# RWKV units in pairs, with one substitution in blocks of 16 for the two of a pair

## The chip, the cores and the metric

The program runs on one core of one Trainium2 chip. The metric is device time in microseconds (us) of one execution. A core has five engines with an instruction queue each, which they work through in order: TensorE (PE, matrix products), VectorE (DVE), ScalarE (ACT), GpSimd (POOL) and SyncE (SP), from which most DMAs are issued. Engines wait for each other by semaphores.

## What is computed

One inference step of a trunk of two layers on 1088 columns: 1024 of a prompt and 8 sequences of 8 samples. Layer 0 mixes by an S5 and a gated DeltaNet, layer 1 by RWKV-7; after each stands a SwiGLU feed-forward part. What matters here is layer 1, cut to this:

```python
def rwkv7_scan(r, decay, k, v, a, b, s0):
    def step(state, inp):
        r_t, w_t, k_t, v_t, a_t, b_t = inp
        sa = jnp.einsum("bhvk,bhk->bhv", state, a_t)
        state = (state * w_t[:, :, None, :] + sa[..., None] * b_t[:, :, None, :]
                 + v_t[..., None] * k_t[:, :, None, :])
        return state, jnp.einsum("bhvk,bhk->bhv", state, r_t)
...
for layer in range(DEPTH):
    ...                       # mixer, then
    x = x + mix.astype(x.dtype)
    h = rmsnorm(x, prm["norm_ffn"][layer])
    x = x + swiglu(h, prm["ffn_w_gate"][layer], prm["ffn_w_up"][layer], prm["ffn_w_down"][layer]).astype(x.dtype)
```

The kernel computes the recurrence in chunks of 64 columns. Within a chunk it needs the inverse of a unit lower triangular 64x64 matrix for each head.

## The kernel before

Every large product goes through `mm` (L322), which splits both factors into a high and a low part and adds three products. The work goes over two halves of the columns. In order of the code: layer 0's first parts, then for each half its tail (output projection `po`, feed-forward products `pg` and `pd`) and layer 1's projections (`pj`); then, for each half, layer 1's output projection and feed-forward tail.

The recurrence of layer 1 is cut into 32 **units** of two heads each: eight head pairs `ft` in four segments `si` of the columns (the last of 320 columns with the samples, the others of 256). I count them in the order of the code, 0 to 31: units 0 to 7 (`si` 0) are called between the projections of the first half, 8 to 15 (`si` 1) behind them, 16 to 23 between those of the second half and 24 to 31 behind. A unit has three parts:

- the **front** (L1550 to L1660): it loads its rows, computes decays, writes `AR`, `BK`, `XV`, `BG` and the chunk matrices `MB`;
- the **inverse** (L155 to L261): the diagonal blocks of 16 are cut out (`D`, L174), go through DRAM (`dA`) into a layout with one block per partition (`L`), are inverted there by a **substitution** of 15 steps with two DVE instructions each (L186, L188), go back through DRAM (`dT`, `Tc`), and from `tt` (L203) on are put together to the inverses `TT` of 64 (last write L259);
- the **back** (L1662 to L1733): for each of four chunks in turn PE, DVE and ACT hand `pa`, `X` (L1685), `pu` and `pb` to each other; then the output `py` is normed to `yo` (L1730) and stored, and read again by the next tail.

Tiles come from pools with a fixed number of buffers. `AR`, `XV`, `BG` and `MB` have two each, so two units can be under way; `TT` has two; the banks `qi` (inverse), `qc` (the back's chunk steps) and `qy` one each. The projections of a half take `qi` and `qc` too (`banks`, L1396).

The order on each engine is set by a scheduler when the kernel is built: it goes by the order of the code and by its own estimate of when inputs are ready. So the units of `si` 1 lie among the tail of the second half of layer 0 (1400 to 2100 us of the profile), and those of `si` 2 and 3 among projections and the tail of layer 1's first half (2330 to 3175 us). On the chip each engine keeps to the order it was given.

Of the kernel before, what the change touches and what calls it, by code (L numbers as in the profile page):

```python
# [8 lines left out]
F32 = mybir.dt.float32  # L9
# [3 lines left out]
OP = mybir.AluOpType  # L13
# [3 lines left out]

T = 1088
NP = 1024
CW = 272  # L20
NCH = [(c, CW) for c in range(0, T, CW)]

# [82 lines left out]
class Kern:  # L105
# [49 lines left out]
    def inverse(self, gp, ps, dr, A, wd, nu, ns, sgn, tag, pb=2, own=False, TT=None):  # L155
# [1 line left out]

        nc, v = self.nc, self.nc.vector  # L160
        nl = 8 * nu + ns
        op = OP.subtract if sgn > 0 else OP.add
        dA = dr.tile([nu + 1, 8, 256], F32, name="dA", tag="dA%d" % wd)
        size = {"mk": 320, "L": 256, "T": 256, "tt32": 160, "Y32": 160}
        kin = {"Y32": "L", "tt32": "T"}
        two = [lambda n, i=i: gp.tile([128, size[kin.get(n, n)] if own else 320], F32, name=n,
                                      tag="i" + kin.get(n, n) if own else "inv%d" % i, bufs=1) for i in range(2)]
        D = gp.tile([128, nu + 1, 16], F32, name="D", tag="invTc", bufs=1 + own)
        for R, n in ((slice(0, 64), nu + 1 if ns else nu), (slice(64, 128), nu)) if wd == 128 else ((slice(0, 128), nu),):
            mk = two[1]("mk").rearrange("p (u b i) -> p u b i", b=4, i=16)[R, 0:n]  # L170
# [4 lines left out]
        nc.sync.dma_start(dA[0:nu].rearrange("u b (j i) -> (b j) u i", i=16), D[:, 0:nu])  # L175
        if ns:
            nc.sync.dma_start(dA[nu, 0:ns].rearrange("b (j i) -> (b j) i", i=16), D[0:16 * ns, nu])
        L = two[0]("L")[:8 * nu + 8, :256].rearrange("p (a b) -> p a b", b=16)
        nc.sync.dma_start(L[:nl], dA.rearrange("u b (j i) -> (u b) j i", i=16)[:nl])
        T = two[1]("T")[:8 * nu + 8, :256].rearrange("p (a b) -> p a b", b=16)  # L180
        v.tensor_copy(T[:nl], self.i16[:nl])
        m = gp.tile([8 * nu + 8, 64], F32, name="Tm", tag="invm", bufs=1)
        for j in range(15):
            n = 15 - j
            mm = m[:nl, :(j + 1) * n].rearrange("p (c i) -> p c i", i=n)
            v.tensor_mul(mm, L[:nl, j:j + 1, j + 1:16].to_broadcast([nl, j + 1, n]),  # L186
                         T[:nl, 0:j + 1, j:j + 1].to_broadcast([nl, j + 1, n]))
            v.tensor_tensor(T[:nl, 0:j + 1, j + 1:16], T[:nl, 0:j + 1, j + 1:16], mm, op=op)  # L188
        dT = dr.tile([nu + 1, 8, 256], F32, name="dT", tag="dT%d" % wd)
        nc.sync.dma_start(dT.rearrange("u b x -> (u b) x")[:nl], T[:nl].rearrange("p c i -> p (c i)"))  # L190
        Tc = gp.tile([128, nu + 1, 16], F32, name="Tc", tag="invTc", bufs=1 + own)
        nc.sync.dma_start(Tc[:, 0:nu], dT[0:nu].rearrange("u b (c i) -> (b c) u i", i=16))
        TS = None
# [16 lines left out]
        C = [slice(32 * b % wd, 32 * b % wd + 32) for b in range(4)]  # L210
# [17 lines left out]
        if TT is None:  # L228
            TT = gp.tile([128, nu, 128], F32, name="TT", tag="invTT", bufs=1)
            nc.gpsimd.memset(TT, 0.0)  # L230
        TT = TT[:, 0:nu]
# [47 lines left out]
    def open(self, ctx, width, tmps, **kw):  # L279

        self.dp = self.dx = ctx.enter_context(self.tc.tile_pool(name="dense", bufs=1, **kw))
        self.width, self.tmps = width, tmps
# [286 lines left out]
class S5:  # L569


    L = 8
    NK = 136
# [632 lines left out]
class RWKV:  # L1206
# [53 lines left out]
    def open(self, ctx):  # L1260

        K, nc, tc = self.K, self.K.nc, self.K.tc
        self.dl = self.dr.tile([288, T], F32, name="dl", bufs=1)
        self.dk, self.drr, self.dv, self.dth, self.dta, self.dg = (
            self.dr.tile([8, 128, T], F32, name=n, bufs=1) for n in ("dk", "drr", "dv", "dth", "dta", "dg"))
        self.dks = {}
        self.ps = ctx.enter_context(tc.tile_pool(name="rps", bufs=2, space=PSUM, side="right"))
        self.gp = ctx.enter_context(tc.tile_pool(name="rww", bufs=2, side="right"))
        self.consts(self.cp)
        self.H = self.cp.tile([128, 8, 64], F32, name="Hs")  # L1270
        nc.gpsimd.memset(self.H, 0.0)

        self.Q = self.cp.tile([128, 4, 2, 64], F32, name="Q")
        nc.gpsimd.memset(self.Q, 0.0)

        self.TT = [self.gp.tile([128, 5, 128], F32, name="TT%d" % i, bufs=1) for i in range(2)]
        self.turn = False
        for t in self.TT:
            nc.gpsimd.memset(t, 0.0)
        self.halo = self.cp.tile([128, 2, 8], F32, name="halo")  # L1280
        nc.vector.memset(self.halo[:, 0], 0.0)

    def projections(self, s, x, shift0, w1, a1, g1, lw2, wk, wr, wv, unit,
                    norms, wk0):

# [152 lines left out]
        for j, wt, dst, more in ((0, wr, self.drr, {1: (0,), 2: (1,), 3: (2, 3), 4: (4, 5), 5: (6, 7)}), (3, wv, self.dv, {})):  # L1438
            hs = [mix(j, i) for i in range(2)]
            if j == 3:  # L1440
                banks = banks[:2]
            for m in range(6):
                w = K.weight(wt[m])
                for i in range(2):
                    one(dst, m, w, hs[i], i)
                for ft in more.get(m, ()):
                    second(ft)
                if j == 3:
                    unit(m)
                if j == 0 and m == 0:  # L1450
                    lora(*loras[5])
                    second = self.second(s, lw2)
                if j == 0 and m == 0:
                    for i, (c, cn) in enumerate(chunks):
                        pt = self.bank("qp")[:16, :cn]
                        for y, (b, n) in enumerate(blocks[i]):
                            nc.tensor.transpose(pt[:, b:b + n], ko[:n, 3 * i + y], K.ident[:n, :n])
                        t = K.tmp("kt")[:16, :cn]
                        nc.scalar.copy(t, pt)
                        nc.sync.dma_start(dks[:, c:c + cn], t)  # L1460
            ws = [K.weight(wt[m]) for m in (6, 7)]
            for i in range(2):
                for m in (6, 7):
                    one(dst, m, ws[m - 6], hs[i], i)
        for m in (6, 7):
            unit(m)
# [68 lines left out]

    def start(self, ft, si, s0, sfin, dy):

        nc, gp = self.K.nc, self.gp
        self.sfin, self.dy = sfin, dy
        S0 = None  # L1540
        if self.SEG[si][2]:
            S0 = gp.tile([128, 8, 64], F32, tag="S0", name="S0", bufs=1)
            nc.sync.dma_start(S0, s0[ft])
        return self.unit(ft, si, si // 2, S0)

    def unit(self, ft, si, s, S0):
        K, nc, gp, HR = self.K, self.K.nc, self.gp, self.HR
        v = nc.vector
        t0, W, smp = self.SEG[si]
        NU, C = 4, 5 if smp else 4  # L1550
        ts = slice(t0, t0 + W)
# [5 lines left out]
        def new(name, tag="up"):  # L1557
            return gp.tile([128, 320], F32, tag=tag, name=name, bufs=RING[tag])[:, :W]
# [64 lines left out]
        pb = ptile("pb")[:, :W]  # L1623
# [7 lines left out]
        MB = gp.tile([128, 5, 64], F32, tag="u_MB", name="MB", bufs=2)  # L1631
        groups = [(0, 4, self.mk)] + ([(4, 1, self.mks)] if smp else [])

        def turned(src, dst):
            for c0, n, mk in groups:
                pt = self.ps.tile([128, 4, 2, 64], F32, tag="q0", name="pt", bufs=2)
                for c in range(n):
                    nc.tensor.transpose(pt[:, c].rearrange("p a t -> p (a t)"),
                                        src[:, c0 + c, 0:2].rearrange("p a t -> p (a t)"), ident)
                nc.scalar.copy(dst[:, c0:c0 + n], pt[:, :n])  # L1640
# [17 lines left out]
                v.tensor_mul(AR[KR, g, hl], pg[KR, :n, 0], mb(KR, 0))  # L1658
                v.tensor_mul(BG[:, g, 1, hl], pg[:, :n, 1], mb(slice(0, 128), 1))
        turned(BK, BG[:, :, 0])  # L1660
        self.turn = not self.turn
        TT, _ = K.inverse(gp, self.ps, self.dr, MB, 64, C, 0, -1.0, "qi", 1, True, self.TT[self.turn])  # L1662

# [4 lines left out]
        pa, pu, pb = pc[:, 0:2], pc[:, 2], pc[:, 3:5]  # L1670
# [7 lines left out]
        two = lambda t: t.rearrange("p a t -> p (a t)")  # L1678
        for u in range(NU):
# [10 lines left out]
            for hl, R in enumerate(HR):  # L1690
                n = XV[R, u + 1, hl] if u + 1 < NU else H[R, NU]
# [29 lines left out]
        for p in parts:  # L1721
            nc.gpsimd.tensor_mul(yc[p], yc[p], wide(rs, p))
            for j in range(p[1].start, p[1].stop):
                n = p[0].stop
# [3 lines left out]
        yo = new("yo", "ul")  # L1728
        v.scalar_tensor_tensor(yo, pT, col(self.lnw), bv, op0=OP.mult, op1=OP.add)
        v.scalar_tensor_tensor(yo, yo, col(self.lnb), g, op0=OP.add, op1=OP.mult)  # L1730
        if si == 3 and ft == 7:
            return yo
        nc.sync.dma_start(self.dy[ft][:, ts], yo)  # L1733

    def sample(self, ft, c, AR, BG, XV, TT, Pe, S0, py):

# [380 lines left out]
```

## Time and profile before

| what | value |
|---|---|
| three runs, median (lowest to highest) | 3689.62 us (3682.62 to 3697.84) |
| the profiled execution, time and span | 3691.23 us, 3689.5 us |
| busy in the span: PE, DVE, ACT, POOL | 92%, 65%, 38%, 28% |
| chain that ended last, by engine | PE 54%, DVE 26%, DMA 12% |

The span is from the first to the last instruction of the profile. A busy PE is not PE at its peak: the records of matmuls that follow each other overlap. An idle engine costs nothing unless the end hangs on it, so the stretches are looked at one by one.

### The profile page before, as it was taken

How to read it: one execution, taken by the hardware profiler on the slowest of the kernel's cores; microseconds unless marked ns; L12 is line 12 of the kernel's file. 1: busy time of each engine (PE TensorE's matmuls, PEld its weight loads, DVE VectorE, ACT ScalarE, POOL GpSimd, SP SyncE). 2: the span in 40 equal slices, each digit the busy share in tenths (PEclk: the TensorE clock that was granted, in tenths of full speed). 3: DMA queues.
4: the chain of work that ended last, by engine and by line, in shares of the span. 5: the costliest groups of instructions: out<-in, count | busy, mean ns of one | idle time of the engine just before them, and what ended most of it. 6: DMA issues, size and time to landing. Idle time of an engine off the chain costs nothing.

```text
span 3689.5 us, 77380 instructions
## 1 busy us (share of the span) xinstructions
PE 3379.0 (92%) x29894; PEld 3171.2 (86%) x29894; DVE 2394.0 (65%) x6834; ACT 1390.8 (38%) x3264; POOL 1041.0 (28%) x1037
## 2 busy tenths in 40 slices
PE   7889999999997889999999898898988989899998
PEld 6879888989997888899889888888887877799997
DVE  7886888754448556776666673577778888344344
ACT  3333333323224454444443454443443444222222
POOL 3222133223216450111010142334333332122221
PEclk8989987999998899999999999989999999899998
DMA  3434453445554585344443456722322324322322
GB/s 102 95 87 120 96 177 104 130 132 188 186 174 132 176 292 161 111 143 150 153 130 114 135 167 221 238 86 87 87 82 84 102 79 135 105 69 75 92 81 66
DMA packets 387552, 474.36 MB, mean 129 GB/s; under 512 B 142312, under 2 KB 305896, under 8 KB 387184
## 3 DMA queue, kind: packets, MB, share of 16 engines
q1 hardware_dynamic: 364144, 447.13, 39.8%
q10 hardware_dynamic: 23040, 22.29, 1.8%
q8 instruction: 235, 3.85, 0.4%
q14 instruction: 133, 1.09, 0.1%
HBM read 344.32 MB, written 123.79 MB: 127 GB/s over the span
## 4 chain that ended last, share of the span: by engine, by line
PE 54%; DVE 26%; DMA 12%; issue 3%; ACT 3%; SPq 1%; POOL 1%; DVEq 0%; ACTq 0%; POOLq 0%
PE pg L322 20%; PE pd L322 10%; PE pj L322 5%; PE po L322 4%; PE pi L322 3%; DVE T L188 3%; DVE Tm L186 3%; DVE mx L1350 1%; DMA raw<-in_wd 1%; DMA dT<-T 1%; DMA L<-dA 1%; DMA rkb<-dks 1%; DMA Tc<-dT 1%; DVE x L534 1%; DVE Z L800 1%
## 5 line engine op out<-in xcount | busy, mean ns | idle before, releaser
L322 PE MATMUL pg<-hi,wh 128*128 128x288 f32 (+1 forms) x2816 | 833.8, 296 | 23.8 <-DVE s L511 15.5
L322 PE MATMUL pg<-lo,wh 128*128 128x288 f32 (+1 forms) x2816 | 830.9, 295 | 4.4 <-DVE lo L409 3.5
L322 PE MATMUL pg<-hi,wl 128*128 128x288 f32 (+1 forms) x2816 | 827.8, 294 | 1.2 <-POOL wl L309 1.2
L309 POOL TENSOR_TENSOR wl<-raw,wh 128x1024 fp32r<-128x1024 f32 (+3 forms) x205 | 483.1, 2358 | 903.5 <-ACT wh L305 791.5
L322 PEld LDWEIGHTS pg<-hi,wh 128*128 128x128 f32 x2816 | 540.7, 192 | 32.9 <-DVE s L511 19.1
L322 PEld LDWEIGHTS pg<-lo,wh 128*128 128x128 f32 x2816 | 540.8, 192 | 12.4 <-DVE lo L409 5.2
L322 PEld LDWEIGHTS pg<-hi,wl 128*128 128x128 f32 x2816 | 540.2, 192 | 3.3 <-POOL wl L309 1.4
L305 ACT CAST wh<-raw 128x1024 fp32r<-128x1024 f32 (+3 forms) x309 | 313.2, 1014 | 362.7 <-PE pg L322 99.6
L322 PE MATMUL pd<-ah,wdh 128*128 128x256 f32 (+1 forms) x1280 | 387.2, 303 | 20.3 <-DVE x L534 16.5
L322 PE MATMUL pd<-ah,wdl 128*128 128x256 f32 (+1 forms) x1280 | 373.5, 292 | 5.9 <-DMA wdl<-low_wd 5.9
L322 PE MATMUL pd<-al,wdh 128*128 128x256 f32 (+1 forms) x1280 | 371.9, 291 | 0.0
L322 PEld LDWEIGHTS pd<-ah,wdh 128*128 128x128 f32 x1280 | 243.8, 190 | 32.0 <-DVE x L534 18.2
L322 PE MATMUL pj<-hi,wh 128*128 128x256 f32 (+1 forms) x768 | 235.5, 310 | 18.1 <-ACT hi L408 7.7
L322 PEld LDWEIGHTS pd<-ah,wdl 128*128 128x128 f32 x1280 | 243.8, 190 | 9.1 <-DMA wdl<-low_wd 7.6
L322 PEld LDWEIGHTS pd<-al,wdh 128*128 128x128 f32 x1280 | 244.2, 191 | 0.4
L322 PE MATMUL pj<-hi,wl 128*128 128x256 f32 (+1 forms) x768 | 232.2, 307 | 12.7 <-DMA wl<-low_wr 7.5
L322 PE MATMUL pj<-lo,wh 128*128 128x256 f32 (+1 forms) x768 | 235.2, 308 | 8.7 <-DVE lo L409 6.8
L534 DVE TENSOR_TENSOR x<-x,pd 128x256 f32<-128x256 f32 (+1 forms) x384 | 162.4, 426 | 92.0 <-PE pd L322 88.5
L305 ACT CAST wdh<-raw 128x384 fp32r<-128x384 f32 (+1 forms) x224 | 111.2, 497 | 258.6 <-PE pd L322 161.2
L322 PE MATMUL pi<-hi,wh 128*128 128x272 f32 x640 | 191.5, 299 | 5.0 <-ACT us L1818 3.5
L186 DVE TENSOR_TENSOR Tm<-L,T 32x15 f32<-32x15 f32 (+8 forms) x600 | 161.1, 268 | 47.6 <-DMA L<-dA 34.6
L322 PE MATMUL pi<-lo,wh 128*128 128x272 f32 x640 | 190.2, 297 | 0.0
(643 smaller groups left out, 8008.2 us busy)
## 6 DMA issues: line engine op xcount, KB each, us to landing
raw<-in_wg SPq DMA_DIRECT2D x88, 512.0 KB
raw<-in_wup SPq DMA_DIRECT2D x88, 512.0 KB
raw<-in_wd SPq DMA_DIRECT2D x192, 192.0 KB
low_wg<-wl SPq DMA_DIRECT2D x22, 512.0 KB
low_wup<-wl SPq DMA_DIRECT2D x22, 512.0 KB
wl<-low_wg SPq DMA_DIRECT2D x22, 512.0 KB
wl<-low_wup SPq DMA_DIRECT2D x22, 512.0 KB
raw<-in_win SPq DMA_DIRECT2D x20, 512.0 KB
```

The costliest lines, as they stand in the source:

```text
L186: v.tensor_mul(mm, L[:nl, j:j + 1, j + 1:16].to_broadcast([nl, j + 1, n]), T[:nl, 0:j + 1, j:j + 1].to_broadcast([nl, j + 1, n]))
L188: v.tensor_tensor(T[:nl, 0:j + 1, j + 1:16], T[:nl, 0:j + 1, j + 1:16], mm, op=op)
L305: nc.scalar.copy(wh, raw)
L309: (lo or nc.gpsimd).tensor_sub(wl, raw, wh)
L322: self.nc.tensor.matmul(ps, a[k], b[:, c:c + cn], start=i == 0, stop=i == last)
L534: v.tensor_add(x[m][:, c:c + cn], x[m][:, c:c + cn], ps)
L800: v.tensor_add(o, o, m1)
L1350: v.scalar_tensor_tensor(t, xx[k][:, c:c + cn], self.vec[:, j, k:k + 1], x[k][:, c:c + cn], op0=OP.mult, op1=OP.add)
```

## The change

`inverse` is cut into `diagonals`, `substitute` and `inverted`; for the DeltaNet the three are called in a row as before. A unit becomes a generator that stops behind `diagonals`. `start` runs the front of an even unit up to there and keeps it; at the odd one it runs that front too, then the rest of the even unit (which does the substitution for both: 64 or 80 partitions in place of 32 or 40) and the rest of the odd one. The pairs are (0, 1), (2, 3) and so on. The numbers of buffers stay as they are.

```diff
         dA = dr.tile([nu + 1, 8, 256], F32, name="dA", tag="dA%d" % wd)
+        self.diagonals(gp, dA, A, wd, nu, ns, own)
+        dT = dr.tile([nu + 1, 8, 256], F32, name="dT", tag="dT%d" % wd)
+        self.substitute(gp, dA, dT, 8 * nu + ns, sgn, own)
+        return self.inverted(gp, ps, dT, A, wd, nu, ns, sgn, tag, pb, own, TT)
...
+    def substitute(self, gp, dA, dT, nl, sgn, own):
...
-        T = two[1]("T")[:8 * nu + 8, :256].rearrange("p (a b) -> p a b", b=16)
+        T = two[1]("T")[:, :256].rearrange("p (a b) -> p a b", b=16)
         v.tensor_copy(T[:nl], self.i16[:nl])
-        m = gp.tile([8 * nu + 8, 64], F32, name="Tm", tag="invm", bufs=1)
+        m = gp.tile([128, 64], F32, name="Tm", tag="invm", bufs=1)
...
     def start(self, ft, si, s0, sfin, dy):
...
-        return self.unit(ft, si, si // 2, S0)
+        unit = self.unit(ft, si, si // 2, S0)
+        next(unit)
+        if ft % 2 == 0:
+            self.other = unit
+            return
+        list(self.other)
+        return next(unit, None)
...
         turned(BK, BG[:, :, 0])
-        self.turn = not self.turn
-        TT, _ = K.inverse(gp, self.ps, self.dr, MB, 64, C, 0, -1.0, "qi", 1, True, self.TT[self.turn])
+
+        if ft % 2 == 0:
+            self.dA, self.dT = (self.dr.tile([2 * C, 8, 256], F32, name=n, bufs=2) for n in ("dA", "dT"))
+        pair, dT = slice(C * (ft % 2), C * (ft % 2) + C), self.dT
+        K.diagonals(gp, self.dA[pair], MB, 64, C, 0, True)
+        yield
+        if ft % 2 == 0:
+            K.substitute(gp, self.dA, dT, 16 * C, -1.0, True)
+        TT, _ = K.inverted(gp, self.ps, dT[pair], MB, 64, C, 0, -1.0, "qi", 1, True, self.TT[ft % 2])
```

In the changed kernel's order lines are numbered anew: L341 is `mm`; L235 to L271 are the inverse's products; L1663 and L1674 are products of the front; L1713, L1718 and L1721 are the back's chunk steps, L1757 its last transposes; L379 and L395 belong to the norm.

PE, end of layer 0's second tail, before. `pd` is the last feed-forward product, `ss` and `bc` are sums for the norm, and `pj` is the first projection of layer 1's second half:

```order
L322 MATMUL pd<-ah,wh 128x288
L322 MATMUL pd<-al,wh 128x288
L322 MATMUL pd<-ah,wl 128x288
L360 MATMUL ss<-sq,one_65 32x72 x32
L376 MATMUL bc<-rst,selq 128x72 x4
L322 MATMUL pj<-hi,wh 128x288 x2
L322 MATMUL pj<-lo,wh 128x288
L322 MATMUL pj<-hi,wl 128x288
```

All units up to 15 stand ahead of these rows. In the changed kernel 48 `pj` stand within 90 rows of the last `pd`, and then come 123 rows without one, of which these are the last, with the 49th `pj` behind them (`py`, `pc` with 128x64 and so on are unit 14's back and, in `py` from 20702 to 20758, unit 15's inverse):

```order
L263 MATMUL py_20564<-t_20519,MB 32x32 x8
L271 MATMUL py_20575<-tt_20557,Y_20563 32x32 x8
L1718 MATMUL pc<-X,TT_13426 128x64
L235 MATMUL py<-t_20702,MB 32x16 x16
L1721 MATMUL pc<-XV,BG 128x128
L239 MATMUL py<-Y_20704,tt 32x16 x16
L1713 MATMUL pc<-XV,AR 128x128
L263 MATMUL py_20747<-t_20702,MB 32x32 x8
L1718 MATMUL pc<-X,TT_13426 128x64
L271 MATMUL py_20758<-tt_20740,Y_20746 32x32 x8
L1721 MATMUL pc<-XV,BG 128x128
L341 MATMUL pj<-hi,wh 128x288
```

What moved: most of the backs of units 10 to 13, and the fronts and inverses of units 12 to 15, stand behind the last `pd`; the 49th `pj` stands behind unit 15's inverse, whose bank `qi` it takes.

PE, end of the tail of layer 1's first half, before. `po` is the output projection of the second half; `pT`, `pk`, `pcr` and `py` are the end of unit 30 and the sample part of unit 31:

```order
L322 MATMUL pd<-ah,wh 128x256
L322 MATMUL pd<-al,wh 128x256
L322 MATMUL pd<-ah,wl 128x256
L360 MATMUL ss<-sq,one_65 32x64 x32
L376 MATMUL bc<-rst,selq 128x64 x4
L1725 MATMUL pT<-ident,yc 128x128 x2
L1725 MATMUL pT<-ident,yc 128x64
L1744 MATMUL pk<-AR,S_34889 64x16 x16
L1750 MATMUL pcr<-ident,rT 64x64 x2
L1761 MATMUL py<-ident,rT 64x128
L376 MATMUL bc<-rst,selq 128x64 x4
L322 MATMUL po<-hi,wh 128x288
```

And now, some 120 rows behind the last `pd` (`pk`, `pcr`, `pcs` are sample parts of unit 29, `py` with x20 are unit 30's inverse):

```order
L1777 MATMUL pk<-AR,S_33190 64x16 x16
L1783 MATMUL pcr<-ident,rT 64x64 x2
L1794 MATMUL py<-ident,rT 64x128
L1789 MATMUL pcs<-XV,AR 64x64 x2
L341 MATMUL po<-hi,wh 128x288 x2
L341 MATMUL po<-lo,wh 128x288
L341 MATMUL po<-hi,wl 128x288
L341 MATMUL po<-lo,wh 128x288
L341 MATMUL po<-hi,wl 128x288
L235 MATMUL py<-t_33440,MB 32x16 x20
L239 MATMUL py<-Y_33442,tt 32x16 x20
L263 MATMUL py_33493<-t_33440,MB 32x32 x10
```

What moved: only unit 31's inverse and back stood behind the last `pd` before; now the inverses and backs of 26 and 27 and all of units 28 to 31 do, with 12 `po` ahead of them and 30 in small groups among them.

## Rows read from the trace of the kernel before

**Rows 1.** Stretches: us, busy us (instructions) of PE, PEld, DVE, ACT, POOL; clock, DMA.

```profile
1479.60:2099.60 620.00, 590.29 (x5694) 558.54 (x5696) 409.19 (x1501) 264.15 (x696) 67.41 (x126) 0.98 0.44 135
2460.00:3125.00 665.00, 607.86 (x6234) 551.84 (x6238) 533.14 (x1635) 279.17 (x757) 248.06 (x239) 0.96 0.30 87
...
3300.00:3400.00 100.00, 100.00 (x758) 100.00 (x757) 39.20 (x69) 27.14 (x46) 28.80 (x12) 1.00 0.29 90
```

**Rows 2.** The same for L322 (PE and PEld alone), two stretches.

```profile
1479.60:2099.60 620.00, 477.48 (x3168) 433.50 (x3168) 0.98 0.44 135
2460.00:3125.00 665.00, 453.24 (x3168) 406.22 (x3168) 0.96 0.30 87
```

**Rows 3.** DVE lines 1479.6 to 2099.6 us, then 2460 to 3125: xcount | busy, mean ns.

```profile
L188 DVE TENSOR_TENSOR T<-T,Tm 32x15 f32<-32x15 f32 (+7 forms) x195 | 38.2, 196 | 4.5
...
L188 DVE TENSOR_TENSOR T<-T,Tm 32x48 f32<-32x48 f32 (+15 forms) x204 | 65.3, 320 | 4.4
```

**Rows 4.** DVE in order of time (start us, us, what): units 10, 12 and 11.

```profile
1781.57 0.82 DVE L1606 TENSOR_TENSOR AR<-r,P 128x256 f32<-128x256 f32 x1
...
1802.11 0.58 DVE L174 TENSOR_REDUCE D<-mk 128x64 f32<-128x256 f32 x1
...
1806.94 0.16 DVE L186 TENSOR_TENSOR Tm<-L,T 32x15 f32<-32x15 f32 x1 [2.96 <-DMA L<-dA]
...
1817.60 0.17 DVE L188 TENSOR_TENSOR T<-T,Tm 32x15 f32<-32x15 f32 x1
...
1823.64 0.29 DVE L203 TENSOR_TENSOR tt<-Tc,half 128x128 f32<-128x128 f32 x1 [2.65 <-DMA Tc<-dT]
...
1836.67 0.58 DVE L259 TENSOR_SCALAR TT<-py 32x128 f32<-32x128 f32 x2
...
1874.69 0.22 DVE L1685 COPY X<-pc 64x64 f32<-64x64 f32 x1 [2.16 <-PE pc L1681]
1874.83 0.41 DVE L1606 TENSOR_TENSOR AR<-r,P 128x256 f32<-128x256 f32 x1
...
1915.92 0.21 DVE L1685 COPY X<-pc 64x64 f32<-64x64 f32 x1
```

**Rows 5.** DVE in order of time: units 1, 17, 24 (its first AR, its last X) and 26.

```profile
1475.83 0.22 DVE L1685 COPY X<-pc 64x64 f32<-64x64 f32 x1
...
2468.86 0.22 DVE L1685 COPY X<-pc 64x64 f32<-64x64 f32 x1 [0.78 <-PE pc L1681]
...
2718.13 0.41 DVE L1606 TENSOR_TENSOR AR<-r,P 128x256 f32<-128x256 f32 x1
...
2812.16 0.21 DVE L1685 COPY X<-pc 64x64 f32<-64x64 f32 x1
2812.29 0.41 DVE L1606 TENSOR_TENSOR AR<-r,P 128x256 f32<-128x256 f32 x1
```

**Rows 6.** DVE in order of time: unit 31, the last.

```profile
3134.47 0.31 DVE L203 TENSOR_TENSOR tt<-Tc,half 128x160 f32<-128x160 f32 x1
...
3148.58 0.65 DVE L259 TENSOR_SCALAR TT<-py 32x160 f32<-32x160 f32 x2 [1.12 <-PE py L252]
...
3158.79 0.22 DVE L1685 COPY X<-pc 64x64 f32<-64x64 f32 x1 [0.89 <-PE pc L1681]
...
3162.85 0.22 DVE L1685 COPY X<-pc 64x64 f32<-64x64 f32 x1 [0.89 <-PE pc L1681]
...
3174.33 0.55 DVE L1730 SCALAR_TENSOR_TENSOR yo<-yo,rvec,g 128x320 f32<-128x320 f32 x1
```

**Rows 7.** PE in order of time, around the ends of the two stretches.

```profile
2099.26 0.29 PE L322 MATMUL pd<-ah,wl 128*128 128x288 f32 x1
...
2122.29 0.29 PE L322 MATMUL pj<-ml,wh 128*64 128x288 f32 x1
...
3124.33 0.28 PE L322 MATMUL pd<-al,wh 128*128 128x256 f32 x1
3124.45 0.28 PE L322 MATMUL pd<-ah,wl 128*128 128x256 f32 x1
```

More of the change, by code (lines that the diff above doesn't have):

```diff
@@ L155, in inverse, with two, diagonals @@
     def inverse(self, gp, ps, dr, A, wd, nu, ns, sgn, tag, pb=2, own=False, TT=None):
-        nc, v = self.nc, self.nc.vector
-        nl = 8 * nu + ns
-        op = OP.subtract if sgn > 0 else OP.add
         dA = dr.tile([nu + 1, 8, 256], F32, name="dA", tag="dA%d" % wd)
+        self.diagonals(gp, dA, A, wd, nu, ns, own)
+        dT = dr.tile([nu + 1, 8, 256], F32, name="dT", tag="dT%d" % wd)
+        self.substitute(gp, dA, dT, 8 * nu + ns, sgn, own)
+        return self.inverted(gp, ps, dT, A, wd, nu, ns, sgn, tag, pb, own, TT)
+    def two(self, gp, own):
         size = {"mk": 320, "L": 256, "T": 256, "tt32": 160, "Y32": 160}
         kin = {"Y32": "L", "tt32": "T"}
-        two = [lambda n, i=i: gp.tile([128, size[kin.get(n, n)] if own else 320], F32, name=n,
-                                      tag="i" + kin.get(n, n) if own else "inv%d" % i, bufs=1) for i in range(2)]
+        return [lambda n, i=i: gp.tile([128, size[kin.get(n, n)] if own else 320], F32, name=n,
+                                       tag="i" + kin.get(n, n) if own else "inv%d" % i, bufs=1) for i in range(2)]
+    def diagonals(self, gp, dA, A, wd, nu, ns, own):
+        nc, v = self.nc, self.nc.vector
+        two = self.two(gp, own)
         D = gp.tile([128, nu + 1, 16], F32, name="D", tag="invTc", bufs=1 + own)
@@ L177, in inverse @@
             nc.sync.dma_start(dA[nu, 0:ns].rearrange("b (j i) -> (b j) i", i=16), D[0:16 * ns, nu])
-        L = two[0]("L")[:8 * nu + 8, :256].rearrange("p (a b) -> p a b", b=16)
+    def substitute(self, gp, dA, dT, nl, sgn, own):
+        nc, v = self.nc, self.nc.vector
+        op = OP.subtract if sgn > 0 else OP.add
+        two = self.two(gp, own)
+        L = two[0]("L")[:, :256].rearrange("p (a b) -> p a b", b=16)
         nc.sync.dma_start(L[:nl], dA.rearrange("u b (j i) -> (u b) j i", i=16)[:nl])
-        T = two[1]("T")[:8 * nu + 8, :256].rearrange("p (a b) -> p a b", b=16)
+        T = two[1]("T")[:, :256].rearrange("p (a b) -> p a b", b=16)
         v.tensor_copy(T[:nl], self.i16[:nl])
-        m = gp.tile([8 * nu + 8, 64], F32, name="Tm", tag="invm", bufs=1)
+        m = gp.tile([128, 64], F32, name="Tm", tag="invm", bufs=1)
         for j in range(15):
@@ L188, in inverse, with inverted @@
             v.tensor_tensor(T[:nl, 0:j + 1, j + 1:16], T[:nl, 0:j + 1, j + 1:16], mm, op=op)
-        dT = dr.tile([nu + 1, 8, 256], F32, name="dT", tag="dT%d" % wd)
         nc.sync.dma_start(dT.rearrange("u b x -> (u b) x")[:nl], T[:nl].rearrange("p c i -> p (c i)"))
+    def inverted(self, gp, ps, dT, A, wd, nu, ns, sgn, tag, pb, own, TT):
+        nc, v = self.nc, self.nc.vector
+        two = self.two(gp, own)
         Tc = gp.tile([128, nu + 1, 16], F32, name="Tc", tag="invTc", bufs=1 + own)
@@ L1276, in open @@
         self.TT = [self.gp.tile([128, 5, 128], F32, name="TT%d" % i, bufs=1) for i in range(2)]
-        self.turn = False
         for t in self.TT:
@@ L1731, in unit @@
         if si == 3 and ft == 7:
-            return yo
-        nc.sync.dma_start(self.dy[ft][:, ts], yo)
+            yield yo
+        else:
+            nc.sync.dma_start(self.dy[ft][:, ts], yo)
     def sample(self, ft, c, AR, BG, XV, TT, Pe, S0, py):
```

## The prediction, made before the result was known

> **What bounds the kernel now.** I read the busy time by stretch first. Two stretches hold the units. In the one from 1479.6 to 2099.6 us (units of `si` 1 among layer 0's second tail) and the one from 2460 to 3125 us (units of `si` 2 and 3 among the tail of layer 1's first half) PE is busy 590 of 620 and 608 of 665 us, DVE 409 and 533 [rows 1]. Each holds 3168 dense products of L322 [rows 2]. In the last stretch, with no units, PE gets 758 products through in 100 us [rows 1], so the first stretch's would take 3168 / 7.58 = 418 us alone; in the second they are 256 columns wide and follow each other every 0.12 us [rows 7], 380 us alone. The rest, 202 and 285 us, is what units cost PE. By the substitution's count (195 and 204 instructions of L188, 15 to a unit [rows 3]) 13.0 and 13.6 units pass, one per 47.7 and 48.9 us, at 15.5 and 21.0 us of PE each.
>
> Then I read DVE in order of time, to see what paces the units. Unit 12 writes `AR` at 1874.83, right behind the last `X` of unit 10 at 1874.69 [rows 4]; units 24 and 26 do the same at 2812.16 and 2812.29 [rows 5]. `AR` has two buffers, and a buffer comes free with the product that this `X` is copied from. So a unit's path from `AR` to its last `X` (93.1 us in unit 10, 94.0 in unit 24) is two unit periods: the units are a chain held by buffers, and the dense products fill PE around it. Both came out even: in the first stretch dense work and units end together, in the second the last `pd` starts at 3124.45 and the last `yo` at 3174.33 [rows 6, 7].
>
> **What goes.** 32 substitutions become 16: 480 DVE instructions fewer in L186 and L188, and 16 `L` and 16 `dT` transfers fewer on SP. At 196 ns in the first stretch and 320 ns in the second [rows 3], with half of them in each, that is 240 x 0.196 + 240 x 0.320 = 124 us of DVE. None of it lies in the way by itself: DVE is not full, and PE does not wait for the substitution but for what the chain delivers. 64 or 80 partitions in place of 32 or 40 I cost at nothing: the copy `X` of 64 columns on 64 partitions takes 0.22 us [rows 4], and the substitution's 0.196 us are for 15 to 64 columns on 32. Were an instruction twice as long on twice the partitions, the 124 us would not be saved, which no step below needs.
>
> **What is added: the chain.** From unit 10 [rows 4] its parts are: front from `AR` to the end of `D` 21.1; through DRAM to the first `Tm` 4.3; substitution 10.8; through DRAM to `tt` 5.9; to the end of `TT` 13.6; to the last `X` 37.4; together 93.1 us. Before, the other unit's parts lay beside these, one buffer each. Now both buffers belong to one pair until its substitution is done. The next pair's odd front needs the `AR` of this pair's odd unit, whose back can only follow the even unit's back (`qc`, `qy` and `H` are single). So a pair's cycle is odd front, substitution for two, inverse, even back, and then the odd back too: 93.1 plus the distance between the last `X` of units 10 and 11, 41.2 us, gives 134 us for two units, where two periods were 93. In the second stretch 94 + 41 = 135. The saved substitution shortens nothing here, since one is on the path in either kernel.
>
> The order bears this out: behind the last `pd` of the first stretch stand about five units more than before, and of the second again about five. This is the term that decides. Five units less among the dense products bring these to an end earlier, but the five then run with nothing beside them.
>
> How fast is an uncovered pair? The trace before has one uncovered back, unit 31: `tt` to the end of `TT` 14.8 us, from there to the last `X` 13.6, a chunk step 4.06 (against about 12 in company) [rows 6]. I take 14 for the inverse, 14 for the first back to its last `X`, 21 for the second (four steps and the change of unit). The substitution with DVE to itself is 30 x 0.196 = 6 us, with 4.3 and 5.9 through DRAM 16. An uncovered front isn't shown: unit 10's 21.1 is the bound above, and half of it, 10, the bound below, as the back shrinks to a third but a front has longer instructions; I take 15. The uncovered cycle is 15 + 16 + 14 + 14 + 21 = 80 us, between 65 (front 10, hand-overs a little shorter) and 98 (front 21, substitution 22, backs 17 and 24, the clock at its lower level).
>
> First stretch. PE alone would reach the last `pd` at 2099 - 5 x 15.5 = 2021 us. The chain says: last `X` of unit 1 at 1475.8 [rows 5], four cycles of 134 to unit 9's, 2012, then 21 + 21 + 14 + 5 to unit 11's `TT`, which stands by the last `pd`: 2073. I take the middle, 2047. From there: last `X` of 10 after 14, of 11 after 21, a cycle of 80, then front, substitution, inverse and the second unit's inverse 15 + 16 + 14 + 5 = 50: 2212. Only then comes the 49th `pj`, which takes the bank `qi` behind unit 15's inverse; before it started at 2122.29 [rows 7]. That is 90 us later. Ends: 2157 (35 later) and 2268 (146 later). The backs of 14 and 15 then cost PE some 30 us among the projections, but the norm ahead of these, which took most of the 23 us from 2099 to 2122, lies beside the units; I set the one against the other.
>
> Second stretch. Last `X` of unit 17 at 2468.9 [rows 5], four cycles of 135: 3009 for unit 25. The odd front and the substitution take 42 there, less as PE runs out of dense work near 3019 (3124 - 5 x 21): `tt` of unit 26 at 3046. Then 14 + 14 + 21 to the last `X` of 27 at 3095, two cycles of 80 to that of 31 at 3255, and 11.5 to its `yo` (as from 3162.85 to 3174.33): 3266, against 3174: 92 us later. Ends: 3213 (39 later) and 3319 (145 later). The last projection hangs on this `yo`, and all that follows is as before.
>
> Sum, against the profiled execution's own 3691.2 us: 3691 + 90 + 92 = 3873 us. That execution lies 1.6 us above the median of the three, which changes nothing here. I forecast 3872 us.
>
> The granted clock is part of this. It was 1.0 of 2.4 GHz where dense work ran alone and 0.96 to 0.98 in the two stretches [rows 1]. The uncovered steps I took from unit 31, which ran partly at 1.2 GHz, so the sum has that already.
>
> A rule speaks against this change: the Trainium skill, in "Perfetto Trace Analysis", section "Identifying Performance Opportunities", says that a gap which repeats on the engine that should be saturated can mean that there is not enough SBUF or PSUM to allocate the next tile (number of buffers). The trace agrees on the cause, since `AR` is written 0.13 us after its buffer's last use. By that rule the two buffers, now held by one pair, are where the time goes; the sum is the same.
>
> **The rivals.** (a) Slower by less: the chain catches up while dense work is there and the uncovered cycle is at its lower end. With the lower ends above: 3691 + 35 + 39 = 3765 us. For it speaks that DVE has 124 us less to do; against it that a front and a back are mostly hand-overs between engines.
>
> (b) Slower by more: an uncovered pair keeps more of its pace in company, as DVE's and ACT's queues still hold the next half's norm and the sample parts: 3691 + 146 + 145 = 3982 us. Against it: unit 31 ran its back at 4.06 us a step with just such company.
>
> (c) Faster: the relief of DVE counts. In the second stretch DVE is busy 80% of the time and PE idle for 57 us [rows 1]; if all of this idle time was for DVE and goes, and the chain's cycle stays hidden, the time is 3691 - 57 = 3634 us. It decides if a pair's cycle stays below two unit periods, 95 us, that is if the odd back can lie beside the next odd front; the one buffer pair of `AR` forbids it, and so does the order. In favour of this stands a rule of the Trainium skill, "VectorE: DVE Perf Modes", section "The TRN2 errata — SBUF-src ops pay a fixed extra latency per instruction": small instructions mostly pay a fixed cost, so fewer of them is what helps. The trace agrees with it for the instruction (196 ns for 15 to 64 columns), not that DVE is what the end waits for.
>
> (d) No change, 3690 us: the pairs lose what the dense products of the next stage cover, as would be if `pj` and `po` were free of the units. They aren't: `pj` waits for `qi`, `po` for `yo`.
>
> **How the numbers follow.** Forecast 0.70, (a) 0.13, (b) 0.12, (c) 0.03, (d) 0.02. The forecast's own range is 3815 to 3930. The whole range goes toward (a) and (b) to 3785 to 3955, which leaves about 2 in 10 outside. Half a per cent is what a measurement here can tell from no change; (a), (b) and the forecast are all slower by more: slower 0.95, same 0.02, faster 0.03.
>
> **What would show it.** In the profile after, the last `X` of the odd unit of a pair is followed at once by the next odd unit's `AR`, and these lie some 130 us apart in the covered stretches; L186 and L188 have 360 instructions each with a mean near the old one. Behind the last `pd` of the first stretch, before 2080 us, PE is mostly idle for 130 to 190 us; the last `yo` of `si` 3 comes more than 200 us after the last `pd` of layer 1's first half. The prediction is wrong if the odd front of a pair starts before the last odd back has read its `AR`, if an uncovered cycle is far from 80 us, or if PE is busy where I see it wait.

## The result, and the profile after

| | before | after |
|---|---|---|
| median (lowest to highest), four runs of each on one chip | 3691.42 us (3682.62 to 3697.84) | 3867.59 us (3861.29 to 3873.02) |
| ratio, 95% interval | 1 | 1.0481 (1.046 to 1.0501) |
| span of the profiled execution | 3689.5 us | 3859.2 us |

The change makes the kernel 4.8% slower. The page of after begins with the busy time of the engines and its share of the span; below, the granted clock in tenths over 40 equal slices:

```profile
PE 3446.0 (89%) x29894; PEld 3212.5 (83%) x29894; DVE 2278.6 (59%) x6338; ACT 1394.1 (36%) x3264; POOL 1044.2 (27%) x1037
...
PEclk9989988999988999999995689989999965699999
```

DVE has 115 us less to do than before (2394.0 us there), and the span is 170 us longer. Two dips of the clock stand in the middle and at three quarters. They lie at the ends of the two stretches with units, as a table by stretch shows (columns as in [rows 1]):

```profile
1472.90:2031.00 558.10, 535.41 (x5026) 512.32 (x5026) 308.78 (x1004) 219.96 (x544) 52.30 (x89) 0.99 0.48 147
2031.00:2196.00 165.00, 90.34 (x776) 70.46 (x777) 109.06 (x369) 57.43 (x173) 48.13 (x84) 0.56 0.09 22
2551.00:3096.00 545.00, 513.06 (x4995) 484.61 (x4996) 354.01 (x1022) 218.91 (x551) 212.57 (x190) 0.97 0.30 89
3096.00:3348.60 252.60, 171.21 (x1592) 120.80 (x1581) 137.84 (x512) 73.68 (x250) 39.25 (x56) 0.58 0.22 65
```

Beside the dense products PE is as full as in [rows 1]. Then come 165 and 253 us in which units run nearly alone: PE is busy for 90 and 171 of them, at 1.2 of 2.4 GHz for most of the time (mean granted clock 0.56 and 0.58).

What paces the units is read from DVE in order of time. This is one covered pair, units 8 and 9, between the last `X` of unit 7 and that of unit 9:

```profile
1848.46 0.21 DVE L1717 COPY X<-pc 64x64 f32<-64x64 f32 x1
1848.60 0.78 DVE L1631 TENSOR_TENSOR AR<-r,P 128x256 f32<-128x256 f32 x1
...
1865.74 0.59 DVE L183 TENSOR_REDUCE D<-mk 128x64 f32<-128x256 f32 x1
1871.49 0.17 DVE L201 TENSOR_TENSOR Tm<-L,T 64x15 f32<-64x15 f32 x1 [2.44 <-DMA L<-dA]
...
1880.16 0.18 DVE L203 TENSOR_TENSOR T<-T,Tm 64x15 f32<-64x15 f32 x1
1887.44 0.29 DVE L222 TENSOR_TENSOR tt<-Tc,half 128x128 f32<-128x128 f32 x1 [4.52 <-DMA Tc<-dT]
...
1900.39 0.58 DVE L278 TENSOR_SCALAR TT<-py 32x128 f32<-32x128 f32 x2
...
1927.62 0.21 DVE L1717 COPY X<-pc 64x64 f32<-64x64 f32 x1
...
1968.25 0.22 DVE L1717 COPY X<-pc 64x64 f32<-64x64 f32 x1 [2.43 <-PE pc L1713]
1968.39 0.41 DVE L1631 TENSOR_TENSOR AR<-r,P 128x256 f32<-128x256 f32 x1
```

Odd unit 9 writes `AR` 0.14 us behind the start of odd unit 7's last `X`, then come front, substitution for both units, the even unit's inverse and back (to 1927.62), the odd back (to 1968.25), and at once the `AR` of odd unit 11. Before, each unit waited so for the unit two ahead [rows 4]; now each pair does, with its two units' backs in a row. The next pairs, partly or wholly behind the last `pd`, look alike but are quicker:

```profile
2087.26 0.22 DVE L1717 COPY X<-pc 64x64 f32<-64x64 f32 x1 [0.89 <-PE pc L1713]
...
2156.46 0.22 DVE L1717 COPY X<-pc 64x64 f32<-64x64 f32 x1 [0.89 <-PE pc L1713]
2156.71 0.81 DVE L1631 TENSOR_TENSOR AR<-r,P 128x256 f32<-128x256 f32 x1
...
2166.70 0.58 DVE L183 TENSOR_REDUCE D<-mk 128x64 f32<-128x256 f32 x1
...
2182.65 0.29 DVE L222 TENSOR_TENSOR tt<-Tc,half 128x128 f32<-128x128 f32 x1 [3.85 <-DMA Tc<-dT]
...
2188.24 0.58 DVE L278 TENSOR_SCALAR TT<-py 32x128 f32<-32x128 f32 x2 [1.32 <-PE py L271]
...
2208.33 0.22 DVE L1717 COPY X<-pc 64x64 f32<-64x64 f32 x1 [3.90 <-PE pc L1713]
...
2224.58 0.22 DVE L1717 COPY X<-pc 64x64 f32<-64x64 f32 x1 [0.37 <-PE pc L1713]
2228.64 0.22 DVE L1717 COPY X<-pc 64x64 f32<-64x64 f32 x1 [0.89 <-PE pc L1713]
```

A covered cycle took 119.8 us here (1848.46 to 1968.25), an uncovered one 72.2 (2156.46 to 2228.64). What waits for it is seen on PE, at the rows that answer to [rows 7]:

```profile
2023.69 0.29 PE L341 MATMUL pd<-ah,wl 128*128 128x288 f32 x1
...
2073.54 0.44 PE L341 MATMUL pj<-hi,wl 128*128 128x288 f32 x1
...
2196.01 0.58 PE L341 MATMUL pj<-hi,wh 128*128 128x288 f32 x1
...
2232.72 0.48 PE L1731 MATMUL py<-XV,BG 128*64 128x64 f32 x4
2233.13 0.61 PE L341 MATMUL pj<-hi,wh 128*128 128x288 f32 x1
...
3095.43 0.28 PE L341 MATMUL pd<-ah,wl 128*128 128x256 f32 x1
...
3348.64 0.61 PE L341 MATMUL po<-hi,wh 128*128 128x288 f32 x1 [1.48 <-ACT hi L427]
```

The last `pd` of the first stretch is 76 us earlier than before, then 48 `pj` run (the last at 2073.54), and the 49th, at 2196.01, starts 122 us behind the 48th. The 121st, at 2233.13, comes right behind unit 15's last `py`. In the second stretch the last `pd` is 29 us earlier and the projection that needs unit 31's output 173 us later (3175.2 before). The rows of DVE for that stretch, which answer to [rows 5, 6], are the odd last `X` of units 17 and 25 to 31 and the last `yo`:

```profile
2567.19 0.21 DVE L1717 COPY X<-pc 64x64 f32<-64x64 f32 x1
...
3062.44 0.21 DVE L1717 COPY X<-pc 64x64 f32<-64x64 f32 x1
...
3167.83 0.22 DVE L1717 COPY X<-pc 64x64 f32<-64x64 f32 x1 [0.34 <-PE pc L1713]
...
3255.21 0.21 DVE L1717 COPY X<-pc 64x64 f32<-64x64 f32 x1
...
3336.63 0.22 DVE L1717 COPY X<-pc 64x64 f32<-64x64 f32 x1 [2.25 <-PE pc L1713]
3347.78 0.55 DVE L1762 SCALAR_TENSOR_TENSOR yo<-yo,rvec,g 128x320 f32<-128x320 f32 x1
```

So the account of the profile is: unit 17's last `X` 2567.19 against 2468.86, 98 us; from there to the last `yo` 780.6 against 705.5 us, 75 more; what follows it is 3.7 us shorter. 98 + 75 - 4 = 169, and the spans differ by 169.7.

### The profile page after: what moved, and what is told of

It reads as the page before. It is cut to its first block, busy times and chain, and to the rows that moved or that the text cites. A ratio compares the mean times of both kernels' runs of the same rounds, so it can differ in the third digit from the quotient of the medians.

```text
span 3859.2 us, 76874 instructions
## 1 busy us (share of the span) xinstructions
PE 3446.0 (89%) x29894; PEld 3212.5 (83%) x29894; DVE 2278.6 (59%) x6338; ACT 1394.1 (36%) x3264; POOL 1044.2 (27%) x1037
## 5 line engine op out<-in xcount | busy, mean ns | idle before, releaser
L341 PE MATMUL pg<-hi,wh 128*128 128x288 f32 (+1 forms) x2816 | 830.0, 295 | 17.9 <-DVE s L530 12.0
L341 PE MATMUL pg<-lo,wh 128*128 128x288 f32 (+1 forms) x2816 | 827.6, 294 | 7.6 <-DVE lo L428 4.5
L341 PE MATMUL pg<-hi,wl 128*128 128x288 f32 (+1 forms) x2816 | 826.6, 294 | 0.8 <-POOL wl L328 0.8
L341 PEld LDWEIGHTS pg<-hi,wh 128*128 128x128 f32 x2816 | 539.7, 192 | 26.2 <-DVE s L530 14.6
L341 PEld LDWEIGHTS pg<-lo,wh 128*128 128x128 f32 x2816 | 539.6, 192 | 11.8 <-DVE lo L428 6.4
L341 PEld LDWEIGHTS pg<-hi,wl 128*128 128x128 f32 x2816 | 539.1, 191 | 3.0 <-POOL wl L328 1.0
L341 PE MATMUL pd<-ah,wdh 128*128 128x256 f32 (+1 forms) x1280 | 383.7, 300 | 16.5 <-DVE x L553 11.0
L341 PE MATMUL pd<-ah,wdl 128*128 128x256 f32 (+1 forms) x1280 | 373.6, 292 | 8.1 <-DMA wdl<-low_wd 5.7
L341 PE MATMUL pd<-al,wdh 128*128 128x256 f32 (+1 forms) x1280 | 371.1, 290 | 0.0
L341 PEld LDWEIGHTS pd<-ah,wdh 128*128 128x128 f32 x1280 | 243.4, 190 | 26.2 <-DVE x L553 10.7
L341 PEld LDWEIGHTS pd<-ah,wdl 128*128 128x128 f32 x1280 | 243.4, 190 | 12.6 <-DMA wdl<-low_wd 8.4
L341 PE MATMUL pj<-hi,wh 128*128 128x256 f32 (+1 forms) x768 | 236.8, 311 | 17.0 <-ACT st L1423 9.2
L341 PE MATMUL pj<-lo,wh 128*128 128x256 f32 (+1 forms) x768 | 237.0, 310 | 13.5 <-DVE lo L428 9.4
L341 PE MATMUL pj<-hi,wl 128*128 128x256 f32 (+1 forms) x768 | 232.9, 307 | 15.7 <-DMA wl<-low_wr 7.1
L341 PEld LDWEIGHTS pd<-al,wdh 128*128 128x128 f32 x1280 | 243.9, 191 | 0.2
L341 PE MATMUL pi<-hi,wh 128*128 128x272 f32 x640 | 192.1, 300 | 7.8 <-ACT pr L1843 5.4
L341 PE MATMUL pi<-lo,wh 128*128 128x272 f32 x640 | 190.6, 298 | 0.0
L341 PE MATMUL pi<-hi,wl 128*128 128x272 f32 x640 | 190.3, 297 | 0.0
```

Of the source, the lines that this page charges most:

```text
L341: self.nc.tensor.matmul(ps, a[k], b[:, c:c + cn], start=i == 0, stop=i == last)
```

## The experiments

Each time is a median, and the ratio is to the kernel before on the same chip, with its interval. "Cuts" are smaller rings elsewhere that make room in SBUF for third buffers; what third buffers are worth is read between kernels with equal cuts.

**The relief of DVE alone.** In the kernel before, odd units leave the substitution out:

```diff
-        nc.sync.dma_start(L[:nl], ...)
+        if not skip:                      # skip: ft % 2 == 1
+            nc.sync.dma_start(L[:nl], ...)
-        for j in range(15):
+        for j in range(0 if skip else 15):
```

> The kernel before, single units in the old order, but the odd units leave out the substitution's 30 DVE instructions and its load (their inverse is built from unit blocks, so their output is not the reference's). This is the gain of the change alone, without its order. Theory T (the loss is that a pair holds both AR buffers until its joint substitution; the relief is small): an odd unit's path is 10 to 13 us shorter, so the chain runs ahead a little and the 50 us behind the last pd of layer 1's first half shrink: 3635 to 3670 us. Rival R (the relief of DVE is worth nothing, or even moves PE's order for the worse): 3690 us or more.

3652.85 us, 0.9905 (0.9873 to 0.9937). What the merge takes off DVE is worth 35 us or so if nothing is added, though DVE is busy 104 us less (2289.7 us in the profile). The change has this relief too, and still takes 176 us more. (Without the substitution the odd units' own paths are shorter too, which speaks for less than 35 us; the order was set anew for this kernel, so that isn't a proven bound.)

**Pairs, each unit with its own substitution.** The order of a pair's parts as in the changed kernel:

```diff
-        if ft % 2 == 0:
-            K.substitute(gp, self.dA, dT, 16 * C, -1.0, True)
+        K.substitute(gp, self.dA[pair], dT[pair], 8 * C, -1.0, True)
```

> The changed kernel, units in pairs, but each unit does its own substitution in 32 or 40 partitions. Order without merging. Behind the last pd of the two stretches some 2.5 and 3.5 units stand in its order, against 5 and 5 in the changed kernel. T: a part of the loss, 3750 to 3800 us, since the even unit's substitution need no longer wait for the odd front. Rival R (the merged substitution itself, with twice the partitions and bytes in its DMAs, is what is slow): 3690 us. Rival S (the order of the code alone does all of it): 3860 us or more.

3767.76 us, 1.0211 (1.0179 to 1.0243). Putting both fronts ahead of both backs costs 2.1%; that the even unit then waits for the odd front to be substituted with it costs the other 2.7%.

**A third buffer for `AR` and `XV`, with cuts.**

```diff
-        RING = {"ui": 6, "up": 5, "ug": 3, "ul": 2}
+        RING = {"ui": 5, "up": 4, "ug": 3, "ul": 2}      # and "uy" 3 to 2, "st" 3 to 2
-        AR = gp.tile([128, 5, 3, 64], F32, tag="u_AR", name="AR")
+        AR = gp.tile([128, 5, 3, 64], F32, tag="u_AR", name="AR", bufs=3)
...
+        XV = gp.tile([128, 5, 2, 64], F32, tag="u_XV", name="XV", bufs=3)
```

The other tiles in these two rings, `ml`, `llo` and `xs`, have three buffers with them.

> The changed kernel with three buffers of AR and XV in place of two; to make room, k/r/v rows have 5 buffers for 6, the front's scratch 4 for 5, the norm's 2 for 3, the projections' staging 2 for 3. T: the next odd front goes on when the even back has ended, a pair's cycle falls from 122 us to some 100, and the time to 3700 to 3780 us, 80 us or more below the kernel with the same cuts and two buffers. Rival R (the merged substitution is slow in itself): no difference from that kernel, about 3870 us.

3734.86 us, 1.0125 (1.0098 to 1.0152). The odd units' last `X` of units 3, 5 and 7 on DVE:

```profile
1582.58 0.21 DVE L1717 COPY X<-pc 64x64 f32<-64x64 f32 x1
...
1677.32 0.21 DVE L1717 COPY X<-pc 64x64 f32<-64x64 f32 x1
...
1774.36 0.21 DVE L1717 COPY X<-pc 64x64 f32<-64x64 f32 x1
```

The cycle is 95 and 97 us here, against 120 or so with two buffers: that is about rival (c)'s condition (95 us), and it comes from buffers alone. In the second stretch the cycles stay longer, 107 us in the mean of four (2472.17 for unit 17 to 2899.28 for unit 25). Unit 17's last `X` is only 3 us later than before [rows 5], so what is left of the loss lies almost wholly in the second stretch.

**The cuts alone, the control of that.** The changed kernel, cuts, two buffers.

> Control for the run with three buffers: the changed kernel with the same smaller rings and two buffers of AR and XV. Both theories: 3860 to 3885 us, as the changed kernel.

3898.37 us, 1.0571 (1.054 to 1.0601), 13 us above what I expected: the cuts cost the paired kernel 31 us. Against this control the third buffers are worth 163 us.

**Pairs in `si` 2 and 3 only.**

```diff
         unit = self.unit(ft, si, si // 2, S0)
+        if si < 2:                       # units 0 to 15 singly, with their own substitution
+            list(unit)
+            return
```

> Pairs only in the second half of the columns (segments 2 and 3); the units of segments 0 and 1 run one by one with a substitution each, as before. Splits the loss by stretch. T: only the second stretch's part, 75 to 90 us, is left: 3765 to 3785 us; the rest (some 75 us up to the 49th pj and some 25 us behind it) is the first stretch's. Rival U (the loss sits in one of the two stretches, say where the samples are): 3690 or 3860 us.

3753.19 us, 1.0201 (1.0182 to 1.0221), 12 us less than expected. The second half's pairs cost 68 us by themselves (3685.14 before, on this chip); that leaves 108 us of the whole change's 176 for the first half. The trace gives 98 and 71, my forecast gave 90 and 92.

**Single units with the third buffers, and with the cuts alone.** The kernel before, with the edits of the third and the fourth experiment.

> The kernel before, units one by one, with three buffers of AR and XV and the smaller rings of the runs before. T: three units share the chain, so its period falls below 46 us until something else holds it, and the 50 us behind the last pd shrink: 3640 to 3690 us, below the kernel before. Rival V (two buffers only cost the pairs; single units are held by PE, and the smaller rings cost 30 us as they did with pairs): 3700 to 3725 us.

> Control: the kernel before with the same smaller rings and two buffers of AR and XV. In its order unit 31 ends at dense product 15528, before 15594. T and V: 3680 to 3725 us.

3674.32 us, 0.9987 (0.997 to 1.0004), and 3661.25 us, 0.9943 (0.9924 to 0.9962). At equal cuts third buffers cost single units 13 us, 0.4%. The first time lies in T's range, but it isn't shown to be below before, as T had it. The chain does run ahead with three buffers (unit 15's last `X` at 2050.11, 34 us earlier than before, the last `yo` at 3140.33, also 34 earlier); what comes behind doesn't end earlier by that, so the chain isn't all that holds single units. That the cuts alone make the kernel faster I had not expected (a miss of 19 us below the range), and it is the quickest whole kernel of these runs. Two rows of its profile answer for most of it, the last `X` and `yo` of unit 31:

```profile
3122.86 0.21 DVE L1685 COPY X<-pc 64x64 f32<-64x64 f32 x1
...
3147.38 0.55 DVE L1730 SCALAR_TENSOR_TENSOR yo<-yo,rvec,g 128x320 f32<-128x320 f32 x1
```

Unit 31 ends its chunk steps 40 us and its `yo` 27 us earlier than in [rows 6], while PE still has `po` to do, and the span is 28.6 us shorter. Smaller rings gave the scheduler another order; which of the four cuts did it wasn't tried.

**The bank `qi`.** In the changed kernel the second half's projections use the two `pa` banks only, so none waits for a unit's bank:

```diff
-        banks = [K.pa, K.pa, lambda n: self.bank("qi"), lambda n: self.bank("qc")]
+        banks = [K.pa, K.pa] + ([] if s else [lambda n: self.bank("qi"), lambda n: self.bank("qc")])
```

> The changed kernel, but the projections of the second half use only the two shared banks, not the inverse's qi nor the chunk steps' qc. In its order the 49th pj stands some 70 rows earlier, ahead of the last pair's inverses. T: the 49th pj starts 30 to 60 us earlier, but the projections soon need the units' other tiles and have two banks where they had four; 3830 to 3870 us. Rival W (the wait for qi is the whole loss of the first stretch): some 75 us less than the changed kernel, 3790 us.

3865.64 us, 1.051 (1.049 to 1.053): nothing is gained. PE around the 49th and the 169th `pj`, and ACT's `mh` ahead of the latter:

```profile
2131.94 0.59 PE L341 MATMUL pj<-hi,wh 128*128 128x288 f32 x1
...
2230.16 0.48 PE L1731 MATMUL py<-XV,BG 128*64 128x64 f32 x4
2230.68 0.76 ACT L427 CAST mh<-mx 128x288 fp32r<-128x288 f32 x2 [2.85 <-PE py L1731]
2232.07 0.47 PE L341 MATMUL pj<-mh,wh 128*64 128x288 f32 x1 [1.44 <-DVE yc L1746]
```

The 49th `pj` starts 64 us earlier than in after, with it 120 run, and the 169th again stands behind unit 15's last `py`, at 2232 us as the 121st of after did. From there on both are alike. So `qi` was only the first door; the end of the chain of units is the second, and it decides. The rows show what is shared there. The 169th `pj` is the first of the small products of `mh` and `ml` that stand among the projections. In the code these take the bank `qy` (L1382), which unit 15's `py` holds until DVE has read it into `yc`, and PE waits 1.44 us for that. And two tiles `mh` take both buffers of `BG`'s ring (L1376), so the second can be written only when unit 15's `py` has read its `BG`; ACT waits for that `py` and writes `mh` 0.04 us behind its end.

**Only `AR` with three buffers, with cuts.**

> The changed kernel with the smaller rings and three buffers of AR alone, XV at two. T as the prediction put it (AR is the ring that paces the chain): as with both, some 3735 us. T with XV as the next ring behind it (a front writes XV right after AR, and XV is held even longer, to the end of the back): 3880 to 3900 us, as with two of each.

3864.81 us, 1.0485 (1.0451 to 1.0519): 34 us of the 163, 15 us below the second expectation, and the covered cycle stays at 121 us. DVE between the last `X` of unit 6 and the `D` of unit 9, with unit 7's last `py` and unit 9's `XV`:

```profile
1802.11 0.21 DVE L1717 COPY X<-pc 64x64 f32<-64x64 f32 x1
1802.24 0.79 DVE L1631 TENSOR_TENSOR AR<-r,P 128x256 f32<-128x256 f32 x1
...
1843.95 0.21 DVE L1717 COPY X<-pc 64x64 f32<-64x64 f32 x1
...
1849.66 0.34 PE L1731 MATMUL py<-XV,BG 128*64 128x64 f32 x4
...
1850.62 0.59 ACT L1665 COPY XV<-pt 128x512 f32<-128x512 f32 x1
...
1857.71 0.58 DVE L183 TENSOR_REDUCE D<-mk 128x64 f32<-128x256 f32 x1
```

Unit 9 has its `AR` at 1802.24, 42 us before unit 7's last `X` at 1843.95, and yet its `D` comes only 14 us behind that `X`. With `AR` free, the next ring of two holds the front. That this ring is `XV` follows from the third experiment, where `XV` at three is the only other edit; here `XV` is written 0.62 us behind the end of unit 7's last `py`, which reads the buffer it needs. `XV` alone at three was not run: that `AR` holds as well is read from its write right behind the last `X`.

**Third buffers, pairs, a substitution per unit.** The third experiment with the edit of the second.

> Three buffers of AR and XV, smaller rings, units in pairs, but one substitution for each unit: the run with three buffers without the merging. T: what is left of the loss there (3735 against 3661 us of single units with the same rings) is the even unit's wait for the odd front, so 3660 to 3700 us. Rival (what is left comes from the order of the code): 3720 us or more.

3687.15 us, 1.0013 (0.9994 to 1.0032): as fast as before. So with three buffers the order of pairs costs some 0.3% against single units with the same rings (1.0013 against 0.9987), and the joint substitution the other 1.1%.

## Why the prediction was right

**The mechanism** is the one named: the units are a chain held by rings of two, a pair fills both buffers, and its cycle is the odd front, the substitution, the inverse and two backs in a row. Order alone costs 2.1%, holding the even unit for the joint substitution 2.7%; with a third buffer in `AR` and `XV` they cost 0.3% and 1.1%. The cycle from unit 3's last `X` to unit 11's follows the same steps: 87 us before, 121 after, 102 with a substitution for each unit, 95 with three buffers, 85 with both. The total of 182 us came out as 170 in the profile, because terms that were too large and terms that were too small nearly cancel; that 3872 us lies so close to 3867.59 is luck.

One of the signs that the prediction named did not come: behind the last `pd` of the first stretch PE was to be mostly idle for 130 to 190 us. The 165 us are there, but PE is busy for 90 of them, at a granted clock of 0.56 in the mean. What the lower clock adds to an uncovered cycle no run shows.

**The covered cycle: 134 forecast, 122 measured** (1480.5 to 1968.25 is four cycles from unit 1 to unit 9, 2567.19 to 3062.44 four of 124 in the second stretch, 135 forecast). Part by part, for unit 9's cycle in us:

| part | forecast | measured |
|---|---|---|
| odd front to the end of `D` | 21.1 | 17.7 |
| through DRAM to the first `Tm` | 4.3 | 5.2 |
| substitution | 10.8 | 8.9 |
| through DRAM to `tt` | 5.9 | 7.1 |
| even unit's inverse | 13.6 | 13.5 |
| even back | 37.4 | 26.7 |
| odd back | 41.2 | 40.6 |

The step that was mis-sized is the even back. Its 37.4 us were read in unit 10, beside another unit's front and inverse; I carried a duration from one company into another. The substitution is shorter since fewer instructions are in DVE's queue between its own: 8, where unit 10's had 17.

**The uncovered cycle: 80 forecast, 69 and 72 in the first stretch, 87 and 81 in the second.** Unit 15's parts from the rows above: front 10.6 (15 forecast), DRAM and substitution 15.4 (16), inverse 6.2 (14), even back 19.5 (14), odd back 20.3 (21). The inverse was read from unit 31, which has the samples' blocks too and ran in company. An uncovered chunk step took 4.06 us (2224.58 to 2228.64), as in [rows 6], both at a granted clock of 0.50, so a step behind the dense products was sized rightly, and the whole parts around it were not.

**First stretch: 90 forecast, 98 measured.** The last `pd` starts at 2024, by the view that PE sets it (2021); the chain's view (2073) and the middle I took (2047) were wrong, since PE runs the dense products ahead wherever the order lets it. The 49th `pj` is 74 us later (90 forecast) against the row at 2122.29 that the prediction took. That row is a product of `ml`; the 49th product of `hi` and `lo`, which answers to the one of after, started at 2126.71 before, so it is 69 us later. The step that failed is what I set to nothing behind it: the norm against the last two backs. In fact the 121st `pj` stands behind unit 15's end: 2233.1 against 2150.4 for the 121st of `hi` and `lo` before, 83 us later, and by layer 1's first `po` it is 98 (2469.43 against 2371.56). I took the first door on the way, `qi`, for the one that decides; the experiment on that bank opened it and gained nothing. The second is seen on ACT in after too, 0.04 us behind the end of unit 15's last `py`:

```profile
2233.24 1.10 ACT L427 CAST mh<-mx 128x288 fp32r<-128x288 f32 x3 [2.84 <-PE py L1731]
```

Before, unit 15's last `py` ended at 2089.4 and the first `mh` was written at 2117.67, so these tiles waited for no unit. No run gave `BG` a third buffer, or the small products another bank. What PE waited for most from 2060 to 2300 us (total, times, longest):

```profile
PE py L235 <- DVE t L227: 24.7, 2, 12.9
```

This is the wait for the blocks that come back through DRAM (`t` is made behind `tt`), which no other work covers there.

**Second stretch: 92 forecast, 75 measured.** Four covered cycles took 495 us instead of 540; from unit 25's last `X` to the last `yo` it took 285 instead of 257, as the pair in the change from covered to uncovered (26 and 27) took 105 where I had 86, and two uncovered ones 169 instead of 160. Dense work lasted 33 us into that pair (3062.44 to 3095.43), where the forecast gave it 10 (3009 to 3019). The errors have opposite signs. The last 11 us, from `X` to `yo`, were as read.

**What goes.** L201 and L203 have 360 instructions each, as forecast. Their means in the two stretches, on twice the partitions (columns as in [rows 3]):

```profile
L203 DVE TENSOR_TENSOR T<-T,Tm 64x15 f32<-64x15 f32 (+7 forms) x75 | 15.1, 201 | 1.6
...
L203 DVE TENSOR_TENSOR T<-T,Tm 64x15 f32<-64x15 f32 (+14 forms) x66 | 18.1, 274 | 1.4
```

So twice the partitions cost next to nothing: 201 ns against 196, and in the second stretch 274 against 320 (why both are higher there stands in the last section). The Trainium skill, "VectorE: DVE Perf Modes", section "The TRN2 errata — SBUF-src ops pay a fixed extra latency per instruction", says that an instruction of VectorE pays a fixed cost, which weighs the more the smaller its operand is. The trace agrees: with 480 instructions fewer, and those of the pairs on twice the partitions, these two lines take 178 us where they took 319; DVE as a whole is busy 115 us less. What that is worth is another matter: some 35 us in the first experiment. The rival built on the rule, (c), named its condition rightly, a pair's cycle of two unit periods, and it takes more buffers. With three it was reached in the first stretch (95 and 97 us) and not in the second (107), and the kernel was not faster but 1.3% slower.

**The rule on repeated gaps** ("Perfetto Trace Analysis" of the Trainium skill, section "Identifying Performance Opportunities": they can mean too few buffers) holds: the third buffers gave back 163 us. But the prediction named `AR` alone, since its write stood right behind the release; giving `AR` alone a third buffer brought 34 of these us. One ring more, `XV`, stood behind it with the same number and nearly the same life, and hid until `AR` was free.

## What to carry to other kernels

Before merging a small step of two iterations, count which buffers both hold until the merged step is done: with a ring of two, a pair that shares one step turns two overlapped chains into one serial chain, and the merge must save more than a whole back. When a ring is seen to hold, list all rings with the same life and the same number, and raise them together; here the first was plain in the trace and the second was not. Look also which rings the work behind shares with the chain: here that work waited for the chain's end, not for the first resource that it freed. And a duration read beside other work isn't carried over to a place with other company.

## What the runs showed of the hardware

The instructions of the substitution took 201 ns on 64 partitions and 196 on 32. In the second stretch they have means of 262 to 274 ns after (320 before), and the longest of L203 in the whole run took 2311 ns, where the shortest took 154 (min, median, max in ns):

```profile
L203 DVE TENSOR_TENSOR T<-T,Tm x360: 154/201/2311, 340.3 to 3285.2; 64x15 f32<-64x15 f32 x12, 64x39 f32<-64x39 f32 x12, 64x55 f32<-64x55 f32 x12, 64x63 f32<-64x63 f32 x12
```

The long ones have POOL beside them. This is the longest:

```profile
2718.34 2.31 DVE L203 TENSOR_TENSOR T<-T,Tm 64x63 f32<-64x63 f32 x1
...
2718.19 2.38 POOL L328 TENSOR_TENSOR wl<-raw,wh 128x1024 fp32r<-128x1024 f32 x1
```

Of the 720 instructions of L201 and L203 in after, 649 run with none of POOL's beside them; they take 197 ns in the mean and 222 at most. Of the other 71, 37 take over 300 ns, and each of these ends within 0.08 us of the end of a POOL instruction. Before it is the same: 1058 without, 193 ns in the mean and 219 at most, and all 83 over 300 ns beside POOL. POOL is busy for 213 of 545 us in the second covered stretch and for 52 of 558 in the first. So the higher means of the second stretch come from this company, not from the columns or partitions. No run changed POOL's work.
